# A hybrid SSD and attention block: z by seven block products, down's weight sums placed anew, other banks in the SSD stage

## The chip, the cores and the metric

One Trainium2 chip, one core of it. The time is that of the device for one execution of the whole kernel, in microseconds (us). Engines: PE (TensorE, matmuls; PEld is its weight load), DVE (VectorE), ACT (ScalarE), POOL (GpSimd), SP (SyncE, which here issues every DMA). The kernel before took 1809.08 us in the median of three runs (1808.15 to 1813.9).

## The reference

One layer of a decoder block on x of 1024 tokens by 1024 channels, in float32. Cut to what matters:

```python
h = rms_norm(x, pre_norm1_w) * (1 + sc1) + sh1
z, xbc, dt_raw, q, k, v, gates = split(h @ w_in)          # z: 1024 columns, dt_raw: 16
y_ssd = ssd_branch(z, xbc, dt_raw, ...)                   # Mamba-2, chunks of 128 tokens, 16 heads of 64
y_att = diff_attention_branch(q, k, v, ...)
merged = sigmoid(g_ssd) * (y_ssd @ w_ssd_o) + sigmoid(g_att) * (y_att @ w_attn_o)
x = x + g1 * rms_norm(merged @ w_out, post_norm1_w)
h2 = rms_norm(x, pre_norm2_w) * (1 + sc2) + sh2
u_gate, u_val = split(causal_dwconv(h2 @ w_up, ...))      # 2 x 2816 columns
x = x + g2 * rms_norm((gelu(u_gate) * u_val) @ w_down, post_norm2_w)

# in ssd_branch: y is the scan of xbc by dt, then
y = y * silu(z)
y = y * rsqrt(mean(y * y, over each of 2 groups of 512) + 1e-5) * norm_w
```

The block z with dt_raw, 1024 tokens by 1040 columns, inner length 1024, is what the first part of the change computes in another way.

## The kernel before, in words

**Arithmetic.** A large product is made in three matmuls: operands are split into a high and a low part (`split`, hi by ACT, lo by DVE's subtraction, L96), and hi·hi, hi·lo and lo·hi are summed in the same bank of PSUM.

**Order.** From the head to the end each of PE, DVE, ACT and SP runs its instructions in the order in which the program emits them (`manual_schedule`). An instruction that waits holds up everything behind it on its engine. On SP that holds for the issues of DMAs too: the issue of a load into a buffer that is still being stored waits for that store, and whatever stands behind it waits as well.

**Stages.** The head (norm of x, the first products) runs to about 92 us. Then come 15 **pairs**, m = 0 to 14, to 378.43 us. A pair makes two blocks of 128 columns of w_in times all tokens as 2x2 blocks in seven products p = 0 to 6 (Strassen, in Winograd's form). The right operands are fixed for all pairs: the four quarters of h and four sums of them (`b11`, `b21`, `t2`, `t1`, `t3`, `b22`, `t4`, in this order), kept split in `HX`. The left ones are weights and four sums of weights (`x_sum`, L406), split by `x_split` (L397 on ACT, L398 on DVE) three products ahead. A product is 12 matmuls of 128x512 (`x_mms`, L422 to L424). It goes to bank X, Z or Y; X is evicted by ACT copies and its sums with the others by DVE (L782, L791, L795). The last product, p = 6, writes into bank X, which L791 must have read. The kinds of the pairs set what else is done: gates (a tanh and a store), rope for q and k (pairs 1 and 3, posted one and two pairs later: swaps of rows by DMA, L468 and L469, and four DVE steps of 128x1024, L471 to L475), and in m = 10 to 14 the SSD input, whose causal convolution follows one pair later as DVE steps of up to 1.28 us (L499) and ACT steps (L496, L501).

**down's weight sums.** The feed-forward's last product uses seven block products too; the sums of its weights are made early, and go back to memory. `down_sums` (L533 to L543) makes four sums of 128x512 for each of 11 blocks of rows, two loads (L529) before and two stores after (L536, L543): 44 sums on DVE, 22 loads and 22 stores on SP. There are two sets of buffers (`wdr`). In the kernel before, 16 sums stand in pairs 10 to 14 (pair 10 after products 3 to 6, the others after 0, 3 and 6) and 28 in the z stage.

**z.** The 1040 columns are cut in thirds (346, 346, 348), and for each third eight tiles of 128 tokens are made by 24 matmuls (`mm3`, L117 to L119), 576 in all. The tokens are PE's stationary side, and the weights' columns move. A tile is evicted by ACT's tanh (L970) and a DVE step (L971) that gives twice silu(z), and is stored (L972); the factor goes into `nwr` and the norm. Beside that run the last pair's convolution, the end of ada (`ada_end`, `ada_turn`), down's sums, and the decays: `decays_a` (softplus of dt, L856 to L882), `decays_b` (cumulative sums by two matmuls, L886 to L893), `decays_c` (transposes of them and their store, L895 to L902).

**SSD.** Sixteen steps u (chunk c, group g). In a step: transposes of the inputs into a pair of banks (`ps_mm`, L1123 to L1134), the decay matrix M loaded (`load_decay`), made on ACT (L1147, L1149) and masked on DVE (L1154), the state's part `pq` (L1161), read by DVE (L1162), and the inner part `py` (L1165), read by DVE (L1167), then the state (`pst`, L1179). Steps later the normed y is turned by four transposes, `ytr` (L1220). Matmuls of v (L1051 to L1053) fill PE between them. Before, `pq` has bank wc, and `py` and `ytr` share bank wb. Attention, the dense part and the feed-forward follow; nothing changes in them but line numbers.

Of the kernel before, what the change touches and what calls it, by code (L numbers as in the profile page):

```python
# [17 lines left out]
P = 128  # L18
D = 1024
# [44 lines left out]
def kernel(ctx: ExitStack, tc: tile.TileContext, a: dict, out: bass.AP, dbg=None):  # L64
# [238 lines left out]
    zd = [dp.tile([P, D], F32, tag=f"zd{i}", name=f"zd{i}") for i in range(8)]  # L303
# [51 lines left out]
    thirds = ((0, 346), (346, 346), (692, 348))  # L355
    z_raw, wz = [], []

    def fetch_z(c0, wdt, kp):
        raw = zraw[:, :, :wdt] if kp == 3 else wp.tile([P, 2, wdt], F32, tag="wraw", name=f"wz{c0}_{kp}_raw", bufs=3)
        SP.dma_start(raw, a["w_zdt"][2 * kp * P : (2 * kp + 2) * P, c0 : c0 + wdt].rearrange("(k p) c -> p k c", p=P))  # L360
        return raw

    def split_z(c0, wdt, kp, raw, own=None):
        if own is not None:
            hi, lo = [t[:, :, :wdt] for t in own]
            split(hi, lo, raw)
            return hi, lo
        hi = wp.tile([P, 2, wdt], F32R, tag="whi", name=f"wz{c0}_{kp}_hi", bufs=4)
        lo = wp.tile([P, 2, wdt], F32R, tag="wlo", name=f"wz{c0}_{kp}_lo", bufs=4)
        split(hi, lo, raw)  # L370
        return hi, lo
# [58 lines left out]
    growt = const("growt", [2 * KD, P])  # L430
# [94 lines left out]

    def down_load(k, i):
        if k < KF:
            r0 = (k + KF * i) * P
            SP.dma_start(wdr[k % 2][i].rearrange("p h c -> p (h c)"), a["w_down"][r0 : r0 + P, :])  # L529

    def down_sums(k):
        (b11, b12), (b21, b22) = [(t[:, 0, :], t[:, 1, :]) for t in wdr[k % 2]]
        V.tensor_tensor(b11, b12, b11, op=ALU.subtract)  # L533
        yield
        V.tensor_tensor(b12, b22, b12, op=ALU.subtract)
        SP.dma_start(wtd[0][:, k, :, :], wdr[k % 2][0])  # L536
        if k > 0:
            down_load(k + 1, 1)
        yield
        V.tensor_tensor(b22, b22, b11, op=ALU.subtract)  # L540
        yield
        V.tensor_tensor(b21, b21, b22, op=ALU.subtract)
        SP.dma_start(wtd[1][:, k, :, :], wdr[k % 2][1])  # L543
        down_load(k + 2, 0)
        yield

    def all_sums():
        for k in range(KF):
            yield from down_sums(k)

    wdr = []
    sums_dn = all_sums()

    EN = mybir.EngineType
    with tc.manual_schedule(engines={EN.PE, EN.DVE, EN.Activation, EN.SP}):
# [199 lines left out]
        for m, (kind, *_) in enumerate(pairs):  # L755
# [6 lines left out]
            for p in range(7):  # L762
# [51 lines left out]
                if (m, p) in ((9, 4), (10, 3)):  # L814
                    wdr.append([SL.get(f"wdr{len(wdr)}{j}", F32, (P, 2, HALF)) for j in range(2)])
                if (m, p) in ((9, 4), (9, 5), (10, 3), (10, 4)):
                    down_load(*divmod(((9, 4), (9, 5), (10, 3), (10, 4)).index((m, p)), 2))
                if p in {10: (3, 4, 5, 6)}.get(m, (0, 3, 6) if m > 10 else ()):
                    next(sums_dn)
                if last:  # L820
                    SL.put(*HX[order[p][0]]) if order[p][0][0] == "t" else None
                    if p == 4:
                        for k in range(KH):
                            hT[k][1] = new_hl(f"b12_{k}")
                            SP.dma_start(hT[k][1].rearrange("p h t -> p (h t)").bitcast(F32), h12d[k])
                    if p == 3:
                        SL.put(*sab)
                    if p == 3:
                        zraw = SL.get("zraw", F32, (P, 2, HALF))
                    z_raw += [fetch_z(*thirds[0], kp) for kp in {1: (0,), 2: (1,), 3: (2, 3)}.get(p, ())]  # L830
                    for _ in range(max(0, p - 4)):
                        wz.append(split_z(*thirds[0], len(wz), z_raw.pop(0)))
# [109 lines left out]
    with tc.manual_schedule(engines={EN.PE, EN.DVE, EN.Activation, EN.SP}):  # L942
        for t_, (c0, wdt) in enumerate(thirds):
# [4 lines left out]
            for i in range(8):  # L948
# [24 lines left out]
                if t_ == 1 and i < 5:  # L973
                    dec = dec or decays_a()
                    for _ in range(6):
                        next(dec, None)
# [1660 lines left out]
```

## Time and profile before

| what | us |
|---|---|
| median of three runs (lowest, highest) | 1809.08 (1808.15, 1813.9) |
| the profiled execution | 1808.36 |
| its span | 1806.5 |
| pairs, with the 15 products of seven | about 92 to 378.43 |
| one pair | 19.05 to 19.10 |
| z | 378.43 to 471.28 |
| SSD | 471.28 to about 645 |

Rows of instructions give the start in us, the duration in us, the engine, the line, the operation, output and inputs, then the size (for PE first the stationary one); in brackets stands how long the engine was idle before it and what released it. PE's rows overlap: the next matmul starts before the modelled end of the last, so PE's pace is read from start to start. DVE's and ACT's rows overlap by a little too when they stand back to back (a sum of 0.69 adds 0.60). Windows give busy us and the instructions of each engine in a stretch.

### The profile page before, as it was taken

How to read it: one execution, taken by the hardware profiler on the slowest of the kernel's cores; microseconds unless marked ns; L12 is line 12 of the kernel's file. 1: busy time of each engine (PE TensorE's matmuls, PEld its weight loads, DVE VectorE, ACT ScalarE, POOL GpSimd, SP SyncE). 2: the span in 40 equal slices, each digit the busy share in tenths (PEclk: the TensorE clock that was granted, in tenths of full speed). 3: DMA queues.
4: the chain of work that ended last, by engine and by line, in shares of the span. 5: the costliest groups of instructions: out<-in, count | busy, mean ns of one | idle time of the engine just before them, and what ended most of it. 6: DMA issues, size and time to landing. Idle time of an engine off the chain costs nothing.

```text
span 1806.5 us, 24511 instructions
## 1 busy us (share of the span) xinstructions
PE 1780.1 (99%) x8749; PEld 1492.9 (83%) x8749; DVE 1362.5 (75%) x2245; ACT 919.8 (51%) x1794; POOL 111.2 (6%) x110
## 2 busy tenths in 40 slices
PE   8999999999999999999999999999999999999998
PEld 6788888899877788888888888888888888888887
DVE  7896888876488777666667877679898888876545
ACT  4454444442456656665555443665554554564532
POOL 0000000000155300000000000100000000000001
PEclk9999999999999999999999999999999999999999
DMA  9565787578877886679952576413232223378754
GB/s 373 174 222 165 254 276 254 181 241 285 263 247 234 251 251 171 183 198 279 262 153 99 178 247 256 157 55 117 96 127 104 100 99 111 122 239 301 238 158 165
DMA packets 165322, 356.18 MB, mean 197 GB/s; under 512 B 16064, under 2 KB 64976, under 8 KB 165200
## 3 DMA queue, kind: packets, MB, share of 16 engines
q1 hardware_dynamic: 165200, 354.62, 59.9%
q8 instruction: 69, 1.13, 0.3%
q14 instruction: 53, 0.43, 0.1%
HBM read 248.83 MB, written 103.62 MB: 195 GB/s over the span
## 4 chain that ended last, share of the span: by engine, by line
PE 54%; DVE 5%; DMA 3%; ACT 3%; issue 1%; SPq 0%; POOL 0%; DVEq 0%; POOLq 0%; ACTq 0%
PE upx L2025 4%; PE upx L2026 4%; PE upx L2024 4%; PE o L1531 2%; PE upy L2025 2%; PE upy L2024 2%; PE upy L2026 2%; PE dx L2416 2%; PE dx L2417 2%; PE dx L2415 2%; PE dy L2417 2%; PE dy L2415 2%; PE dy L2416 2%; PE mix L2087 1%; PE mix L2085 1%; PE mix L2086 1%
## 5 line engine op out<-in xcount | busy, mean ns | idle before, releaser
L2024 PE MATMUL upx<-t,wu_t 128*128 128x512 f32 x264 | 103.1, 391 | 0.5 <-DVE cv L2480 0.4
L2025 PE MATMUL upx<-t,wu_t 128*128 128x512 f32 x264 | 102.8, 390 | 0.2 <-DVE t L2142 0.2
L2026 PE MATMUL upx<-t,wu_t 128*128 128x512 f32 x264 | 102.7, 389 | 0.0
L1456 DVE CUSTOM_DVE_ANT_0 sc<-sc,mw 128x256 f32<-128x256 f32 (+7 forms) x128 | 96.2, 772 | 8.6 <-PE sc L1469 7.2
L1998 ACT ACTIVATE wu_t<-sab 128x512 fp32r<-128x512 f32 x57 | 34.1, 627 | 127.7 <-DVE sab L2015 127.7
L1519 ACT COPY aT<-at 128x512 f32<-128x512 f32 (+2 forms) x96 | 45.9, 478 | 95.8 <-PE at L1518 95.6
L96 DVE TENSOR_TENSOR g_lo<-gst,g_hi 128x1024 fp32r<-128x1024 f32 (+1 forms) x42 | 47.5, 1134 | 49.5 <-ACT g_hi L95 49.0
L1531 PEld LDWEIGHTS o<-vt,aT 128*128 128x128 f32 x576 | 76.0, 191 | 5.6 <-ACT aT L1519 0.2
L1531 PE MATMUL o<-vt,aT 128*128 128x128 f32 x576 | 79.9, 275 | 0.0
L95 ACT ACTIVATE g_hi<-gst 128x1024 fp32r<-128x1024 f32 (+1 forms) x42 | 41.5, 990 | 66.1 <-DMA gst<-gld_s 38.3
L397 ACT ACTIVATE xw_t<-xsab 128x512 fp32r<-128x512 f32 x45 | 27.3, 627 | 93.5 <-DVE xsab L406 93.5
L422 PE MATMUL xx<-xt,xw_t 128*128 128x512 f32 x180 | 70.1, 390 | 0.0
L424 PE MATMUL xx<-xt,xw_t 128*128 128x512 f32 x180 | 70.0, 389 | 0.0
L423 PE MATMUL xx<-xt,xw_t 128*128 128x512 f32 x180 | 70.0, 389 | 0.0
L1468 PE MATMUL sc<-kst,qst 128*128 128x512 f32 (+2 forms) x192 | 66.1, 352 | 0.0
L1506 DVE RECIPROCAL rsm<-ssum 128x2 f32<-128x2 f32 x64 | 10.6, 166 | 72.8 <-ACT p L1497 39.6
L1469 PE MATMUL sc<-klo,qst 128*128 128x512 f32 (+2 forms) x192 | 63.3, 346 | 0.4 <-DMA klo<-kld 0.4
L2042 DVE SCALAR_TENSOR_TENSOR ug<-cg,vec,ug 128x1023 f32<-128x1023 f32 (+1 forms) x44 | 56.3, 1280 | 6.1 <-ACT ug L2041 5.3
L2002 DVE TENSOR_TENSOR wu_t<-sab,wu_t 128x512 fp32r<-128x512 f32 x57 | 39.3, 690 | 26.5 <-ACT wu_t L1998 26.5
L2024 PEld LDWEIGHTS upx<-t,wu_t 128*128 128x128 f32 x264 | 49.6, 188 | 11.7 <-DVE cv L2480 1.4
L2025 PEld LDWEIGHTS upx<-t,wu_t 128*128 128x128 f32 x264 | 49.6, 188 | 10.7 <-DVE t L2142 0.5
L1510 DVE SCALAR_TENSOR_TENSOR p<-p,coef,p 128x512 f32<-128x512 f32 (+2 forms) x96 | 56.5, 617 | 2.3
(580 smaller groups left out, 5794.8 us busy)
## 6 DMA issues: line engine op xcount, KB each, us to landing
adas<-in_w_ada SPq DMA_DIRECT2D x32, 512.0 KB, 6.2
wdr<-in_w_down SPq DMA_DIRECT2D x22, 512.0 KB, 4.9
wtd<-wdr SPq DMA_DIRECT2D x22, 512.0 KB, 3.6
wuf<-in_w_up SPq DMA_DIRECT2D x22, 512.0 KB, 3.5
gld_s<-gsum SPq DMA_DIRECT2D x22, 512.0 KB, 2.7
gst<-gld_s SPq DMA_DIRECT2D x20, 512.0 KB, 4.6
wdt_raw<-wtd SPq DMA_DIRECT2D x20, 512.0 KB, 4.9
wuv<-in_w_up SPq DMA_DIRECT2D x19, 512.0 KB, 3.6
```

The lines of the kernel that those rows point to most:

```text
L422: T.matmul(o, wh, xh_, start=(k == 0 and first), stop=False, skip_group_check=not first)
L423: T.matmul(o, wh, xl_, start=False, stop=False, skip_group_check=not first)
L424: T.matmul(o, wl, xh_, start=False, stop=(k == KH - 1), skip_group_check=not first)
L1456: V.tensor_tensor_reduce(out=sc, in0=sc, in1=mw[:, S - L :], scale=1.0, scalar=3.0e38, op0=ALU.add, op1=ALU.min, accum_out=col)
L1468: T.matmul(sc[:, n0:n1], qs_[s][:, tsl], ks_[s][:, n0:n1], start=True, stop=False)
L1531: T.matmul(po_of[j, grp][:, qi, :], at[:, k, :], vt[j % 2][:, kt, :], start=(kt == 0), stop=(kt == i))
L2024: T.matmul(out_, wh, xh_, start=(k == 0 and first), stop=False, skip_group_check=not first)
L2025: T.matmul(out_, wh, xl_, start=False, stop=False, skip_group_check=not first)
L2026: T.matmul(out_, wl, xh_, start=False, stop=(k == end), skip_group_check=not first)
L2415: T.matmul(o, gh[:, kk, tsl], wh, start=(k == 0 and not more), stop=False, skip_group_check=more)
L2416: T.matmul(o, gh[:, kk, tsl], wl, start=False, stop=False, skip_group_check=more)
L2417: T.matmul(o, gl[:, kk, tsl], wh, start=False, stop=(k == KF - 1), skip_group_check=more)
```

## The change

Three things.

**z in seven products.** The 1040 columns are two halves h, and each half is two groups g of 260 columns. For each group the four blocks of weights (half of the inner length by half of the columns), `a11` to `a22`, are loaded (`z_load`), four sums made on DVE (`z_sum`, 128x1040 each), and seven operands split (`z_split`). The token side is the seven operands in `HX` that the pairs leave behind, so it needs no sums. A product is 4 tiles of 128 tokens by 12 matmuls, so 2 × 7 × 48 = 672 matmuls of 260 columns take the place of 576 of 346 or 348. Banks: X and Y of four each, exchanged between the groups; ACT copies what is to be added (`z_keep`), DVE adds it to the other bank (`z_out`), and ACT's own silu gives the result, straight from PSUM for the last. dt is taken from the first 16 columns. Product 3 of the second group is made in two parts, with product 4's first two tiles between them. Exact silu makes the factor in `nwr` and in the norm go. Silu and Exp are of different tables, so there are more table loads: 4 more of them stand in this stage.

**down's sums anew.** Twelve in pairs 3 to 5, eighteen in pairs 10 to 14 (pair 10 after products 2 to 5, 11 to 13 after 1 to 4, 14 after 1 and 2), fourteen in z. In pairs 3 to 5 one set of buffers does, and in pairs 10 to 14 too.

**SSD.** `ytr` has bank wc, which was `pq`'s, and `pq` has a bank of the pair `ps_mm`. M's first three loads, `xch`'s loads and v's first splits are made in the z stage; the first load of z stands a little later, and the quarter of h that `HX` doesn't hold (b12) is loaded again at the end of z.

The diff, cut to its core:

```diff
+    down_at = {(2, 4): "l", (2, 6): "l", (3, 2): "s", (3, 3): "s", (3, 4): "s", (3, 5): "l", (3, 6): "s", (4, 0): "l", (4, 1): "s", (4, 2): "s", (4, 3): "s"}
+    down_at |= {(4, 4): "ls", (4, 5): "l", (4, 6): "s", (5, 0): "s", (5, 2): "s", (5, 4): "s"}
...
+    for m in (11, 12, 13):
+        down_at |= {(m, 1): "s", (m, 2): "s", (m, 3): "s", (m, 4): "ls", (m, 5): "l"}
...
-                if p in {10: (3, 4, 5, 6)}.get(m, (0, 3, 6) if m > 10 else ()):
-                    next(sums_dn)
+                down(down_at.get((m, p), ""))
...
+    def z_mms(g, p, qs=range(4)):
+        n, bk = order[p]
...
+        wh, wl = zop[7 * g + p]
+        for q in qs:
+            o = zbank[g, bk, q]
+            tsl = slice(q * P, (q + 1) * P)
+            for k in range(KH):
+                xh_, xl_ = HX[n][k][:, 0, tsl], HX[n][k][:, 1, tsl]
+                T.matmul(o, xh_, wh[:, k, :], start=(k == 0 and first), stop=False, skip_group_check=not first)
+                T.matmul(o, xh_, wl[:, k, :], start=False, stop=False, skip_group_check=not first)
+                T.matmul(o, xl_, wh[:, k, :], start=False, stop=(k == KH - 1), skip_group_check=not first)
...
+    def z_out(g, h, half, bk, e, o):
+        t = zout[o]
...
+            if e is None:
+                A.activation(t[:, q, :], zbank[g, bk, q], AF.Silu)
+            else:
+                V.tensor_tensor(t[:, q, :], zbank[g, bk, q], zev[e][:, q, :], op=ALU.add)
...
+        z_mms(1, 2)
+        z_keep(1, "X", 1)
+        assert next(dec, None) is None
+        decays_b()
+        z_split(12)
...
+        down("sss")
+        v_raw.append(fetch_v(0, 2))
+        z_mms(1, 3, (0, 1))
+        decays_c()
+        z_mms(1, 4, (0, 1))
+        z_keep(1, "Y", 0, (0, 1))
+        z_mms(1, 3, (2, 3))
...
-            pq = ps_wc(f"pq{c}_{g}")
+            pq = ps_mm(f"pq{c}_{g}")[:, 0, :]
...
-                turn_y(*divmod(u - 3, 2))
+                turn_y(*divmod(u - 3, 2), ps_wc)
```

Two places of DVE's order show what the list `down_at` and the new z stage do. The first is the second half of pair 13, from the sum of weights in product 1 to the eviction of bank X before product 6; `wdr` are down's sums, `xw_t` and `xw_b` the splits of weights, `xbcT` the convolution's steps, `xsab` the sums of weights, `xcg` and `xcv` the evictions. Before:

```order
L406 TENSOR_TENSOR xsab_797<-xwf_2533,xwv_2640 128x512
L398 TENSOR_TENSOR xw_t_2779<-xsab_797,xw_t_2779 128x512
L499 SCALAR_TENSOR_TENSOR xbcT_2761<-xcg_889,vec,xbcT_2761 128x1022
L782 TENSOR_TENSOR xcg_697<-xz_2743,xevs_888 128x512
L398 TENSOR_TENSOR xw_b_2798<-xsab_797,xw_b_2798 128x512
L499 SCALAR_TENSOR_TENSOR xbcT_2761<-xcg_889,vec,xbcT_2761 128x1021
L398 TENSOR_TENSOR xw_t_2816<-xwv_2640,xw_t_2816 128x512
L499 SCALAR_TENSOR_TENSOR xbcT_2819<-xcv_890,vec,xbcT_2819 128x1023
L542 TENSOR_TENSOR wdr_2275<-wdr_2275 128x512
L398 TENSOR_TENSOR xw_b_2838<-xwf_2677,xw_b_2838 128x512
L499 SCALAR_TENSOR_TENSOR xbcT_2819<-xcv_890,vec,xbcT_2819 128x1022
L791 TENSOR_TENSOR xcv_698<-xx_2742,xevs_888 128x512
```

And now, from the sum of product 1 (L540's first row here) on:

```order
L540 TENSOR_TENSOR wdr_2293<-wdr_2293 128x512
L792 TENSOR_TENSOR xcg_690<-xz_2763,xevs_881 128x512
L403 TENSOR_TENSOR xw_b_2818<-xsab_790,xw_b_2818 128x512
L503 SCALAR_TENSOR_TENSOR xbcT_2781<-xcg_882,vec,xbcT_2781 128x1021
L540 TENSOR_TENSOR wdr_2293<-wdr_2294,wdr_2293 128x512
L403 TENSOR_TENSOR xw_t_2838<-xwv_2656,xw_t_2838 128x512
L503 SCALAR_TENSOR_TENSOR xbcT_2841<-xcv_883,vec,xbcT_2841 128x1023
L540 TENSOR_TENSOR wdr_2294<-wdr_2294,wdr_2293 128x512
L403 TENSOR_TENSOR xw_b_2858<-xwf_2696,xw_b_2858 128x512
L503 SCALAR_TENSOR_TENSOR xbcT_2841<-xcv_883,vec,xbcT_2841 128x1022
L540 TENSOR_TENSOR wdr_2294<-wdr_2294 128x512
L801 TENSOR_TENSOR xcv_691<-xx_2762,xevs_881 128x512
```

Between the convolution's step of 1022 and the eviction there was one sum; now there are four, one after each of products 1 to 4.

The second place is DVE around the decays' end in z: `acum_ps` is the bank of the cumulative sums, `acs` the copies of their transposes, `wz` splits of z's weights. Before:

```order
L889 COPY sm_3039<-acum_ps 128x128
L892 TENSOR_TENSOR sm_3039<-acum_ps,sm_3039 128x128
L535 TENSOR_TENSOR wdr_2274<-wdr_2275,wdr_2274 128x512
L540 TENSOR_TENSOR wdr_2275<-wdr_2275,wdr_2274 128x512
L96 TENSOR_TENSOR wz_1_lo<-wz_1_raw,wz_1_hi 128x696
L96 TENSOR_TENSOR wz_2_lo<-wz_2_raw,wz_2_hi 128x696
L96 TENSOR_TENSOR wz_3_lo<-zraw,wz_3_hi 128x696
L971 SCALAR_TENSOR_TENSOR ev_3041<-ev_3041,z_7_3601 128x346
L542 TENSOR_TENSOR wdr_2275<-wdr_2275 128x512
L971 SCALAR_TENSOR_TENSOR ev_3042<-ev_3042,z_0_3644 128x348
```

And now:

```order
L889 SCALAR_TENSOR_TENSOR sm_3051<-sm_3051,aexp 128x128
L368 TENSOR_TENSOR wza_3261<-zxr,wza_3259 128x1040
L96 TENSOR_TENSOR wz1t_lo<-wza_3261,wz1t_hi 128x1040
L896 COPY sm_3051<-acum_ps 128x128
L899 TENSOR_TENSOR sm_3051<-acum_ps,sm_3051 128x128
L96 TENSOR_TENSOR wz1b_lo<-wza_3323,wz1b_hi 128x1040
L540 TENSOR_TENSOR wdr_2293<-wdr_2294,wdr_2293 128x512
L540 TENSOR_TENSOR wdr_2294<-wdr_2294,wdr_2293 128x512
L540 TENSOR_TENSOR wdr_2294<-wdr_2294 128x512
L908 COPY acs<-acT_ps_3763 16x512
```

The copy of `acum_ps` stands behind a sum and a split of 1040 columns, and the copies of the transposes behind a split and three sums of down; before, they stood several tiles of z apart. (The last row is the first of the two copies.)

More of the change, by code (lines that the diff above doesn't have):

```diff
@@ L547, in all_sums, with down_sum @@
[L547 to L552, printed above, removed]
+        r0 = (k + KF * i) * P
+        SP.dma_start(wset(k)[i].rearrange("p h c -> p (h c)"), a["w_down"][r0 : r0 + P, :])
+    def down_sum(k, i):
+        (b11, b12), (b21, b22) = [(t[:, 0, :], t[:, 1, :]) for t in wset(k)]
+        o, x_, y_ = ((b11, b12, b11), (b12, b22, b12), (b22, b22, b11), (b21, b21, b22))[i]
+        V.tensor_tensor(o, x_, y_, op=ALU.subtract)
+        if i % 2 == 1:
+            SP.dma_start(wtd[i // 2][:, k, :, :], wset(k)[i // 2])
@@ L1006 @@
+    assert n_ada == 32 and n_dn == 4 * KF
+    SL.put(*HX["t4"], *zev, *zout, zxr, *wdr[0], *wdr[1])
     singles.close()
@@ L1012 @@
     GW = HALF
-    RH = NH // 2
-    M = [SL.get(f"M{n}", F32, (P, RH, P)) for n in range(3)]
     yt = [SL.get(f"yt{i}") for i in range(3)]
```

311 lines of the change are left out of this document (181 added, 130 removed).

## The prediction

> **What bounds the kernel now.** I read the page's busy shares first, then the groups of waits on PE by stretch, then windows for the stretches that the change touches, then single rows.
>
> ```profile
> span 1806.5 us, 24511 instructions
> PE 1780.1 (99%) x8749; PEld 1492.9 (83%) x8749; DVE 1362.5 (75%) x2245; ACT 919.8 (51%) x1794; POOL 111.2 (6%) x110
> ```
>
> PE is busy 99% of the span, so time falls only where PE gets less work or loses one of its few waits. The waits of PE from the z stage into attention, as PE's line, what it waited for, total us, times, longest:
>
> ```profile
> PE ytr L1220 <- DVE yt L1167: 4.1, 3, 2.1
> PE py L1165 <- DVE M L1154: 0.6, 1, 0.6
> PE v L1052 <- DVE wv_lo L920: 0.4, 1, 0.4
> ```
>
> That is 5.1 us in the SSD stage. The pairs and z have none. Three windows follow: z, a late pair (m=13) and an early one (m=4). The columns are the stretch, its length, then busy us and instructions of PE, PEld, DVE, ACT, POOL, the granted clock, the DMA share and GB/s:
>
> ```profile
> 378.43:471.28 92.85, 92.85 (x591) 92.46 (x590) 56.36 (x108) 25.89 (x46) 0.00 (x0) 1.00 0.84 281
> 340.33:359.38 19.05, 19.05 (x85) 15.70 (x84) 17.07 (x24) 10.17 (x15) 0.00 (x0) 1.00 0.59 185
> 168.60:187.70 19.10, 19.10 (x86) 15.83 (x85) 13.10 (x18) 6.36 (x11) 0.00 (x0) 1.00 0.44 133
> ```
>
> In z, DVE works 56 of 93 us; in a late pair it works 17.1 of 19.05. So z has room on DVE and the late pairs have next to none, and the change takes sums out of z and puts two of them into pairs. That the clock is 1.00 everywhere leaves it out of what follows. The profiled execution took 1808.36 us, 1.9 outside its span; it lies 0.7 below the median of the runs shown (1809.08) and 0.2 above the lowest. I count from 1808.36. About 0.3%, 5.4 us, is what a measurement of this kernel can tell from no change: below 1802.9 is faster, above 1813.8 slower.
>
> **A. PE's work in z.** 576 matmuls of 346 or 348 columns go, 672 of 260 come.
>
> ```profile
> 378.43 0.32 PE L117 MATMUL z<-wz_hi,hT 128*128 128x346 f32 x1
> 471.12 0.32 PE L119 MATMUL z<-wz_hi,hT 128*128 128x348 f32 x1
> 749.26 0.28 PE L1468 MATMUL sc<-kst,qst 128*128 128x256 f32 x1
> 749.38 0.28 PE L1469 MATMUL sc<-klo,qst 128*128 128x256 f32 x1
> 749.50 0.40 PE L1468 MATMUL sc<-kst,qst 128*128 128x512 f32 x1
> ```
>
> Durations overlap, so what counts is the step from start to start. In z it is (92.85 − 1.5)/576 = 0.1586 us, with about 1.5 us for the 15 other PE instructions (591 − 576: transposes and sums of ada and the decays, at some 0.1 us each). No row shows 260 columns; 256 columns step 0.12 (749.26, 749.38, 749.50), 346 columns 0.1586. By the slope between these, 0.0004 a column, 260 would be 0.1217; by the 256-wide rows in proportion 0.1219; read to their two digits, 0.118 to 0.123. I take 0.120, since rounding hides a few ns: 672 × 0.120 = 80.6 us (79.3 to 82.7). With the same 1.5 that is 82.1, or −10.7 before any wait.
>
> The product (14,6), of twelve 512-wide matmuls, goes from 375.71 to 378.43 (the rows below), 0.2267 each. The Trainium skill, TensorE: Matmul & The Clock Gate, section "Wait — 56ns, not 53.3ns?", gives N ÷ 2.4 GHz and about 2.5 ns from start to start, which is 0.216 for 512 columns, 0.147 for 346 and 0.111 for 260; the sum by it would have 74.5 us instead of 80.6. The rows here are 5 and 8% above it, so the measurement decides.
>
> **B. New waits in z.** Before, z needs from DVE only weight splits and evictions with whole tiles to spare. After, PE's 12-matmul groups stand in one order with transposes of the decays, whose inputs stand on DVE behind splits, and with banks that DVE must empty. Prices of what stands in the queues, on DVE and ACT:
>
> ```profile
> 461.64 1.22 DVE L920 TENSOR_TENSOR zown<-wv_raw,zown 128x1024 fp32r<-128x1024 f32 x1
> 495.38 0.42 DVE L1086 TENSOR_TENSOR was<-was 128x256 f32<-128x256 f32 x1
> 448.85 1.27 DVE L901 COPY acs<-acT_ps 16x512 f32<-16x512 f32 x2
> 413.01 0.46 ACT L970 ACTIVATE ev<-z 128x346 f32<-128x346 f32 x1 [0.71 <-PE z L119]
> 413.49 1.28 ACT L858 ACT_TABLE_LOAD   x1
> 414.78 0.31 ACT L858 ACTIVATE sm<-sm 128x128 f32<-128x128 f32 x1
> ```
>
> DVE's sum there is no bound: 22 splits and sums of 1040 columns at 1.22, 24 adds of 260 at 0.42 and 14 down sums at 0.69 make 47 us; with the last conv steps and the decays some 70 of 86. The waits are of order. Product 3 of the second group is cut in two, and its tiles 2 and 3 take the banks of the two transposes. Their copies (1.27 together) stand behind a weight split (1.22) and three down sums (3 × 0.60 in a row): 4.3 us on DVE from the moment the subtraction before them is done. PE has tiles 0 and 1 of product 4 to do meanwhile, 24 × 0.12 = 2.9. That leaves 1.4, with hand-over 1.6. The transposes before them wait for the copy of acum, which stands behind a 1040-wide sum and split: 1.0; the second half of the decays' chain runs over ACT, where table loads of 1.28 now stand: 1.0. The cumulative sums wait 0.4 for la, the ada transposes 0.3 for gcol. Sum 4.3. Lower bound 1, if DVE runs ahead by one split (1.2) at each of them; upper bound 7, if it is a split late at each of two. A + B: −6.4, from −11 to −2.
>
> The trace shows the load at 413.49 start 0.02 after the ACTIVATE before it ended and last 1.28, and the next operation follows at 414.78: 1.3 us a switch. The Trainium skill, ScalarE: Activation LUTs, section "What ACT_TABLE_LOAD costs", gives about 1283 ns and about 1380 ns of drain for each switch; the load agrees, and no row here shows a drain.
>
> **C. Down's sums in pairs 11 to 14.** There were three in a pair (products 0, 3, 6); now four (products 1 to 4), and two in pair 14.
>
> ```profile
> 339.12 0.69 DVE L795 TENSOR_TENSOR xcg<-xy,xevs 128x512 f32<-128x512 f32 x1
> 341.71 0.69 DVE L535 TENSOR_TENSOR wdr<-wdr,wdr 128x512 f32<-128x512 f32 x1
> 344.18 1.28 DVE L499 SCALAR_TENSOR_TENSOR xbcT<-xcg,vec,xbcT 128x1023 f32<-128x1023 f32 x1 [0.58 <-ACT xbcT L496]
> 355.76 0.68 DVE L791 TENSOR_TENSOR xcv<-xx,xevs 128x512 f32<-128x512 f32 x1
> 358.76 0.69 DVE L795 TENSOR_TENSOR xcg<-xy,xevs 128x512 f32<-128x512 f32 x1
> 374.80 0.69 DVE L791 TENSOR_TENSOR xcv<-xx,xevs 128x512 f32<-128x512 f32 x1
> 375.71 0.39 PE L422 MATMUL xx<-xt,xw_t 128*128 128x512 f32 x1
> ```
>
> PE's last product of a pair reuses the bank that L791 (L801 after) empties. In pair 13 the eviction ends at 356.44, and PE starts that product at 359.38 − 2.72 = 356.66: 0.22 to spare. In pair 14 it ends at 375.49 against 375.71: 0.22 again. DVE's own period is 358.76 − 339.12 = 19.64 against PE's 19.05, so in pair 12 there was 0.8 to spare and in pair 11 1.4: DVE falls behind by 0.6 a pair already, and nobody notices until it has used its lead. After, the sum at 341.71, which lay in front of a wait for ACT of 0.58 anyway, is gone, and two sums stand where DVE never waits: 2 × 0.60 = 1.2 more a pair, a period of 20.85. Pair 11 uses up its lead of 1.4. By pair 12 DVE is 2 × 1.2 = 2.4 later, less some 0.5 that it still idled for ACT in pair 11, against 0.8: PE waits 1.1. From then on the bound is DVE's period: 20.85 − 19.05 = 1.8 in pair 13. Pair 14 has two sums and no longer the third, but one split of z's weights (1.15) stands before the eviction: 1.15. Sum +4.1; less if ACT's lag eats the sums (3), 5 if every sum counts. The cover that is gone is DVE's lead; once PE is stalled, what is late next is z's second product, whose split stands behind the same row; PE has 5.8 us of product 0 before that.
>
> **D. Sums in pairs 3 to 5.** Twelve sums, six loads and six stores are put among the swaps, stores and weight loads of the rope pair on SP. The first three rows are of DVE, the next two are groups of DMAs with count, KB each and us from issue to landing; then the spread of the loads and of everything on that tile:
>
> ```profile
> 168.42 0.69 DVE L398 TENSOR_TENSOR xw_t<-xsab,xw_t 128x512 fp32r<-128x512 f32 x1 [0.70 <-ACT xw_t L397]
> 178.46 0.69 DVE L398 TENSOR_TENSOR xw_t<-xwv,xw_t 128x512 fp32r<-128x512 f32 x1 [2.58 <-ACT xw_t L397]
> 183.08 0.68 DVE L791 TENSOR_TENSOR xcv<-xx,xevs 128x512 f32<-128x512 f32 x1
> wdr<-in_w_down SPq DMA_DIRECT2D x22, 512.0 KB, 4.9
> wtd<-wdr SPq DMA_DIRECT2D x22, 512.0 KB, 3.6
> DMA to landing us min/median/max: 4.1/4.9/7.3
> DMA to landing us min/median/max: 2.8/4.5/8.2
> ```
>
> There is only one set of buffers here, so a block's second load follows its predecessor's store. The last sum of block 0 ends at 169.7 (behind the row at 168.42), its store lands 3.6 later, 173.4, SP issues the load behind it at 173.9, it lands at 178.8. DVE comes to sum (4,2) at about 175.9, in the 2.58 that it idled before 178.46, so it stands there 2.9, and rope's three steps of 1.22 and the eviction of 183.08 are behind it. That eviction ended at 183.76, and PE's product 6 starts at 187.70 − 2.72 = 184.98, so 1.2 of the 2.9 is covered; some of the rest the later idle time takes. PE waits 0.4 to 1.2 there, and 0 to 2.5 in pair 5, where an eviction on ACT stands behind rope's copy and that behind DVE. Swap DMAs issue up to 3 us later, behind the down load that waits; rope's steps follow them. I take +1.5, from 0 (the loads land at 4.1 and the idle time holds all) to 4. Pairs 10 and z's own loads have two products' time, 5.4 us, or more after the store.
>
> **E. SSD's banks.** The rows are of PE, DVE and ACT:
>
> ```profile
> 517.39 0.66 PE L1220 MATMUL ytr<-ident,yt 128*128 128x128 f32 x4 [2.06 <-DVE yt L1167]
> 558.51 0.66 PE L1220 MATMUL ytr<-ident,yt 128*128 128x128 f32 x4 [1.42 <-DVE yt L1167]
> 589.38 0.66 PE L1220 MATMUL ytr<-ident,yt 128*128 128x128 f32 x4 [0.67 <-DVE yt L1167]
> 515.45 0.68 DVE L1162 TENSOR_TENSOR tt<-pq,sm 128x512 f32<-128x512 f32 x1
> 516.65 0.68 DVE L1167 TENSOR_TENSOR yt<-py,yt 128x512 f32<-128x512 f32 x1
> 478.81 1.28 ACT L1147 ACTIVATE M<-M,sm 128x128 f32<-128x128 f32 x4 [3.40 <-DMA M<-acd]
> ```
>
> ytr waits for L1167 because it takes py's bank; the data that it turns are two steps older. With the wc bank it needs none of this. pq now stands in the mm pair, which L1162 frees 1.2 us ahead of L1167, so the next user of the pair can wait for that where ytr waited: 2.06 − 1.2 = 0.9 in the worst of the three, 1.42 − 1.2 = 0.2 in the next, nothing in the last; but v's matmuls stand between in some steps, so 0.4. M's loads are issued in z, so ACT's 3.40 and PE's 0.6 behind it go, and the 0.4 of v too. −4.1 + 0.4 − 0.6 − 0.4 = −4.7, from −5.1 to −2.5 (M stays, and a half of ytr's wait moves to the pair).
>
> **Sum.** −6.4 + 4.1 + 1.5 − 4.7 = −5.5: 1808.4 − 5.5 = 1802.9, written 1803.0.
>
> **The rivals.** *PE alone bounds.* If sums and new waits find idle time after all (C at 0, D at 0, B at 1), −9.7 − 4.7 gives 1794; with one of the three still there 1796 to 1799. For it: DVE's busy share is 75%. Against it: 0.22 us of slack in two late pairs. Chance 0.22.
>
> *Shorter steps at 260 columns.* By the figure of the page on TensorE above, 6.1 less than my sum: 1797; the 512- and 346-wide rows speak against it: 0.04.
>
> *DVE takes PE's place.* C 5, D 4, B 6: −4.7 + 5 + 4 − 4.7 = −0.4, 1808. For it: the period of 19.64 in the late pairs. Against: that 75%. 0.17.
>
> *A drain at each table switch.* Two of the new loads stand on the way of the decays; if ACT paused after each as long again as its load, 1.3, the transposes would be 2.6 later: 1805.5. The page on ScalarE above names such a drain; the row at 414.78 speaks against it: 0.03.
>
> *Down's loads come late (slower).* Each block's second load waits for a store to land. At the longest landings, 8.2 and 7.3, a block has 15.5 us between sum and sum, where pairs 4 and 5 leave 6 and pairs 11 to 13 about 13. Then DVE stands 9 us at each of two blocks, 18, of which idle time and lead take some 6, so D is 12 instead of 1.5; and 2.5 at each of three blocks of the late pairs, where no lead is left, 7.5. Together 18 over the forecast: 1821. It turns slower than before at 11 us over the forecast, 2.2 us for each of the five. For it: nothing but those maxima; the medians, 4.9 and 3.6, leave only D's 2.9. 0.08.
>
> That the change doesn't do what it says I leave out: the program has the 672 matmuls.
>
> **How the numbers follow.** Forecast 0.46, half of it on either side of 1802.9 (own range 1799 to 1807). So faster 0.23 + 0.22 + 0.04 = 0.49; same 0.23 + 0.17 + 0.03 = 0.43; slower 0.08. The range, 1795 to 1811, leaves out the late loads and a third of the case of PE alone.
>
> **What would show it.** Right: 260-wide steps of 0.12, z at 84 to 88 us, PE waits at product 6 of pairs 12 to 14 of 1 to 2 us each for L801, one at pair 4 or 5, ytr's wait gone. Wrong: no wait in the late pairs (C falls), a z of 82 (B falls) or over 90, waits on wdr's loads of over 3 us in pairs 10 to 13, or new waits on the mm pair of over 2 us.

## The result and the profile after

The changed kernel takes 1831.58 us in the median of five runs (1830.73 to 1835.97), the kernel before 1809.24 (1808.15 to 1813.9): a ratio of 1.0124, interval 1.011 to 1.0139. The forecast was 1803. The profiled execution took 1830.73, its span:

```profile
span 1828.9 us, 24673 instructions
PE 1798.2 (98%) x8845; PEld 1485.6 (81%) x8845; DVE 1377.8 (75%) x2248; ACT 935.9 (51%) x1814; POOL 111.7 (6%) x110
```

PE is busy 18 us more than before, though the z stage was to take 10 us of work from it. So the first question is not which wait came, but where PE's work got longer. I set the starts of the same matmuls in the two traces side by side and took the growth of each stretch, in us:

| stretch | before | change |
|---|---|---|
| up to the first pair | 92.55 | +0.46 |
| pairs 0 to 3 | 76.40 | +1.16 |
| pairs 4 to 6 | 57.12 | +5.41 |
| pairs 7 to 11 | 95.20 | +1.77 |
| pairs 12 and 13 | 38.12 | +2.87 |
| pair 14 and z | 111.89 | −5.51 |
| SSD, to the last ytr | 173.08 | +1.37 |
| attention | 354.43 | −1.41 |
| dense part to the feed-forward | 167.53 | +3.11 |
| feed-forward, to the last matmul | 633.66 | +13.30 |

The feed-forward, in which no instruction changed, is 13.3 us longer, and the pairs 7 to 9, unchanged too, are about 0.4 longer each. Here are 100 us of the feed-forward, as in the windows of the prediction. Before:

```profile
1310.00:1410.00 100.00, 100.00 (x443) 82.80 (x442) 86.62 (x114) 52.23 (x77) 0.00 (x0) 1.00 0.31 109
```

And after:

```profile
1310.00:1410.00 100.00, 100.00 (x433) 80.99 (x433) 86.59 (x114) 49.04 (x73) 0.00 (x0) 1.00 0.32 113
```

Both rows say 100 us busy and a clock of 1.00, and no wait. Only the count differs: 443 matmuls before, 433 after. From start to start the 512-wide ones take 0.2267 us before and 0.2318 after on average, 2.2% more. It is so from the first pair (0.231) to the end, with one exception: in attention the 512-wide matmuls of the dense products that fill PE take 0.2303 before already (0.2319 after), and attention isn't longer. It is not in any list of waits, since a matmul that takes longer counts as busy. The waits that the trace does list for PE, from the groups of the whole span:

```profile
...
PE v L1157 <- ACT zout L988: 2.9, 1, 2.9
PE xx L427 <- DVE xcv L801: 2.4, 3, 1.0
PE xx L427 <- ACT xevs L795: 2.4, 1, 2.4
PE pq L1262 <- DVE prev L1282: 1.4, 1, 1.4
...
PE acT_ps L907 <- DVE sm L899: 1.1, 1, 1.1
...
PE acT_ps L907 <- DVE sm L896: 0.9, 1, 0.9
...
PE z L975 <- DVE acs L908: 0.2, 1, 0.2
```

ytr's wait for L1167 is gone, and so is the one for M, as forecast; the pairs and z have the waits that terms B to D spoke of; and the SSD stage has two new ones, 2.9 us for ACT's last silu of z and 1.4 for DVE's sum of the state.

### The profile page after: what moved, and what is told of

It reads as the page before. It is cut to its first block, busy times and chain, and to the rows that moved or that the text cites. A ratio compares the mean times of both kernels' runs of the same rounds, so it can differ in the third digit from the quotient of the medians.

```text
span 1828.9 us, 24673 instructions
## 1 busy us (share of the span) xinstructions
PE 1798.2 (98%) x8845; PEld 1485.6 (81%) x8845; DVE 1377.8 (75%) x2248; ACT 935.9 (51%) x1814; POOL 111.7 (6%) x110
## 3 DMA queue, kind: packets, MB, share of 16 engines
q8 instruction: 70, 1.15, 0.3%
## 4 chain that ended last, share of the span: by engine, by line
PE 65%; DVE 3%; ACT 2%; DMA 1%; issue 1%; POOL 0%; DVEq 0%; SPq 0%; POOLq 0%; ACTq 0%
PE upx L2124 4%; PE upx L2123 4%; PE upx L2122 4%; PE o L1629 3%; PE dx L2515 2%; PE dx L2514 2%; PE dx L2513 2%; PE upy L2124 2%; PE upy L2123 2%; PE upy L2122 2%; PE dy L2515 2%; PE dy L2513 2%; PE dy L2514 2%; PE at L1616 2%; PE mix L2185 1%; PE mix L2184 1%
## 5 line engine op out<-in xcount | busy, mean ns | idle before, releaser
L2122 PEld LDWEIGHTS upx<-t,wu_t 128*128 128x128 f32 x264 | 49.6, 188 | 12.2 <-DVE cv L2578 0.6
L2123 PEld LDWEIGHTS upx<-t,wu_t 128*128 128x128 f32 x264 | 49.6, 188 | 12.0 <-DVE t L2240 0.5
L2124 PEld LDWEIGHTS upx<-t,wu_t 128*128 128x128 f32 x264 | 49.6, 188 | 11.6
```

The lines of the kernel that those rows point to most:

```text
L2122: T.matmul(out_, wh, xh_, start=(k == 0 and first), stop=False, skip_group_check=not first)
L2123: T.matmul(out_, wh, xl_, start=False, stop=False, skip_group_check=not first)
L2124: T.matmul(out_, wl, xh_, start=False, stop=(k == end), skip_group_check=not first)
```

## The experiments

**What slows PE.** Two theories. The first: where the operands lie. A weight tile of z is 4 × 260 × 4 = 4160 bytes a partition, and the pools give each buffer of a tag the size of its largest tile. So the 11 weight buffers, and five of the 43 slots behind them, grow by 64 bytes, and everything behind each moves. In the program as built, all that PE reads for a 512-wide matmul (all but 4 of some 6,400) began, before, at one residue of its address modulo 512, and now at many residues, 64 bytes or a multiple of it apart. The rival: the new instructions themselves, or the load that they put on the chip. One kernel takes the bytes away from the changed kernel (z256), two give them to the kernel before (pad_all, pad_raw).

z256:

```diff
-    ZW = (D + NH) // 4
+    ZW = 256
...
+        if (g, h) == (1, 1):
+            SP.dma_start(zdh[half][:, :, D - NH :], t[:, :, ZW - NH :])
```

> The changed kernel with groups of 256 columns instead of 260; it leaves out the last 16 columns of z and stores a copy of other columns there. Every operand tile is 4096 bytes a partition again, so all tiles begin at one residue of the address modulo 1024, as before the change; everything else stays. Theory 1 (the 64 bytes by which the 4160-byte tiles push their neighbours cost PE a slower step, 0.2317 us instead of 0.2267 a 512-wide matmul, everywhere): about 1800 to 1806 us, with the step back at 0.2267 in the pairs and in the feed-forward. Rival (the slower step comes with the new instructions, their number or the load they put on the chip): 1829 us, the step stays at 0.232, since only 672 x 4 columns, about 1 us, are left out.

Measured: 1812.23 us (8 runs, 1810.2 to 1815.37) beside 1808.3 for the kernel before on this chip, a ratio of 1.0022 (1.001 to 1.0034). The same 100 us:

```profile
1310.00:1410.00 100.00, 100.00 (x443) 82.85 (x442) 87.26 (x117) 51.18 (x75) 0.00 (x0) 1.00 0.32 113
```

The step is back, with 672 new matmuls still there. The time is some 6 us over what I expected of it, which the waits below account for.

pad_all, the opposite (the same for the tags of the high and low parts):

```diff
-        t = xw[n, m] = wp.tile([P, 2, KH, P], F32, tag="wraw", name=f"xw{n}{m}", bufs=3)
+        t = xw[n, m] = wp.tile([P, 1040], F32, tag="wraw", name=f"xw{n}{m}", bufs=3)[:, :D].rearrange("p (n k c) -> p n k c", n=2, c=P)
```

> The kernel before with the tiles of the three weight tags (raw, high, low) made 4160 bytes instead of 4096, which nothing reads, and two small constants placed in a tile that exists; no instruction changes. Theory 1 (addresses): step 0.230 to 0.232 us, 1825 to 1838 us. Rival (new instructions): 1808 to 1810 us, step 0.2267.

Measured: 1828.06 us (two runs), ratio 1.011 (1.0081 to 1.014), no instruction added:

```profile
1310.00:1410.00 100.00, 100.00 (x436) 81.65 (x435) 86.56 (x114) 48.12 (x72) 0.00 (x0) 1.00 0.32 111
```

So the bytes alone do it, and the rival falls.

pad_raw makes only the three raw buffers larger:

> The kernel before with only the three raw weight tiles made 4160 bytes: nearly all that PE reads moves by 192 bytes together and keeps one residue modulo 1024 (896 instead of 704). If theory 1 holds because the operands no longer share a residue: no change, 1808 to 1810 us, step 0.2267. If it is the residue itself that counts: about 1830 us. Rival (new instructions): 1808 to 1810 us.

Measured: 1808.23 us, step 0.2267. Everything was moved by 192 bytes, but together. It isn't the residue that counts, but that it is shared.

**How much must be shared.** Two kernels that compute all of z, and differ only in the size of the 260-column tiles. Room came from constants that were put into tiles that exist (the masks, the rows for lambda, four small ones).

```diff
-        hi = wp.tile([P, KH, ZW], F32R, tag="whi", name=f"wz{g}{n}_hi", bufs=4)
+        hi = wp.tile([P, 1088], F32R, tag="whi", name=f"wz{g}{n}_hi", bufs=4)[:, : KH * ZW].rearrange("p (k c) -> p k c", c=ZW)
```

The low parts and the five slots are made so too; in aligned128 1056 stands for 1088.

> The changed kernel whole, all 1040 columns, with its 260-column tiles given 4352 bytes (17 x 256) instead of 4160, so that every operand of PE begins at one residue modulo 256 again; room for it comes from constants placed in tiles that exist. Theory 1 (a tile's address relative to the others sets PE's step, and a residue shared modulo 256 is enough): step 0.2265 to 0.228 us, 1810 to 1815 us. If only a residue shared modulo 1024 helps: step 0.231, about 1830 us. Rival (the 260-column matmuls themselves slow everything): about 1830 us.

> The kernel with aligned tiles, at 4224 bytes (33 x 128) instead of 4352, so that operands share a residue modulo 128 but not modulo 256; no instruction changes. If the residue modulo 256 is what PE's step hangs on: step 0.229 to 0.232 us, 1822 to 1832 us. If modulo 128 is enough: 0.2267, 1811 to 1815 us.

Measured: aligned 1813.09 us (10 runs), ratio 1.0025 (1.0015 to 1.0036); aligned128 1830.67 in one run. Their windows, first aligned:

```profile
1310.00:1410.00 100.00, 100.00 (x443) 82.88 (x442) 87.27 (x116) 49.95 (x74) 0.00 (x0) 1.00 0.31 108
```

And aligned128:

```profile
1310.00:1410.00 100.00, 100.00 (x434) 81.25 (x433) 86.99 (x114) 50.58 (x75) 0.00 (x0) 1.00 0.31 111
```

With tiles of 4352 bytes, 17 × 256, the step is whole; with 33 × 128 it is lost. The change was 22.3 us slower than before, aligned is 4.5, each against the kernel before on its own chip: 17.8 us are this. What all five kernels of this kind move is tiles, which PE reads and the other engines and the DMAs read and write. That PE's own reads are what counts is the likeliest reading, not shown by itself; the last section has what speaks for it.

**The rest: what is left of the change at the old pace.** aligned is still those 4.5 us slower than before, where the forecast had −5.4. The 256-column kernel shows the waits at the old pace. Its groups of waits for PE, from 100 to 500 us:

```profile
PE xx L427 <- DVE xcv L801: 4.1, 3, 1.8
PE xx L427 <- ACT xevs L795: 2.9, 1, 2.9
PE z L975 <- DVE acs L908: 1.7, 1, 1.7
PE acT_ps L907 <- DVE sm L899: 1.1, 1, 1.1
PE acT_ps L907 <- DVE sm L896: 0.5, 1, 0.5
...
```

Three kernels undo one place each. z256_early (the twelve sums of pairs 3 to 5 left out):

```diff
-    down_at = {(2, 4): "l", (2, 6): "l", (3, 2): "s", (3, 3): "s", (3, 4): "s", (3, 5): "l", (3, 6): "s", (4, 0): "l", (4, 1): "s", (4, 2): "s", (4, 3): "s"}
-    down_at |= {(4, 4): "ls", (4, 5): "l", (4, 6): "s", (5, 0): "s", (5, 2): "s", (5, 4): "s"}
...
+        for k in range(6):
+            SP.dma_start(wtd[k % 2][:, k // 2, :, :], wdr[1][k % 2])
```

> The 256-column kernel (it leaves out 16 columns of z) without the twelve sums of down in pairs 3 to 5, their loads and stores; it leaves those sums out and stores other rows in their place at the end of z. Theory (term D is 3 us or more, since loads and a slot wait for stores to land): PE's waits of 2.9 us in pair 5 and 1.8 in pair 6 go, start of z 4 to 5.5 us earlier than in the 256-column kernel, 1805 to 1808 us in all. Rival (PE's time there is lost to the rope steps anyway): start of z at most 1 us earlier.

z256_late (it loads the next block's rows one sum too early, so some of down's sums are of other rows; the work is the same):

```diff
-    for m in (11, 12, 13):
-        down_at |= {(m, 1): "s", (m, 2): "s", (m, 3): "s", (m, 4): "ls", (m, 5): "l"}
-    down_at |= {(14, 1): "s", (14, 2): "s"}
+    down_at |= {(m, p): "s" for m in (11, 12, 13, 14) for p in (0, 3, 6)}
+    down_at |= {(11, 5): "l", (12, 1): "l", (13, 0): "sl", (13, 4): "l", (14, 2): "l"}
...
+        down("l")
...
+        down("ss")
```

> The 256-column kernel with down's sums in pairs 11 to 14 at products 0, 3 and 6, as before the change, and the two sums that are then over put into z. Theory (term C: two sums more a pair on DVE's path, 4.1 us): the three waits on the last product of pairs 12 to 14, 4.1 us, shrink to under 0.5, z starts 3.5 to 4.5 us earlier. Rival (DVE is late because of pairs 3 to 10 or of z's own splits): at least 2 us of the waits stay.

z256_order:

```diff
         decays_b()
-        z_split(12)
...
-        down("sss")
...
         decays_c()
+        z_split(12)
+        down("sss")
         z_mms(1, 4, (0, 1))
```

> The 256-column kernel with one weight split and three of down's sums put behind the copies of the decays' transposes instead of ahead of them. Theory (term B: the copies queue behind them): the wait of 1.7 us of z's matmuls for the copies goes, z 1.5 to 2 us shorter. Rival (the wait then moves to the split, or the transposes' own waits for acum of 1.1 and 0.5 grow): z shorter by less than 0.5.

Measured: 1813.12, 1810.97 and 1811.3 us, one run each. The first is above the 1805 to 1808 expected of it, for a reason that comes with the SSD stage; the totals say little, the growth over before by stretch does:

| stretch | z256 | early | late | order |
|---|---|---|---|---|
| up to the first pair | +2.46 | +0.23 | +0.06 | +2.47 |
| pairs 4 to 6 | +5.38 | 0.00 | +6.96 | +6.80 |
| pairs 12 and 13 | +2.98 | +3.00 | −0.02 | +2.96 |
| pair 14 and z | −6.21 | −6.22 | −5.63 | −8.17 |
| SSD | −1.77 | +7.65 | −1.44 | −1.11 |

The first two edits take their own places to nothing, the third takes 2.0 off z: the early sums cost 5.4 to 7.0, the late ones 3.0 in two pairs, the copies' queue 2.0. Where the early sums cost more than 5.4, the clock differs too: where pairs 4 to 6 lost 6.8 or 7.0 us (order 6.8, late 7.0, and 6.8 in aligned), the granted clock was 0.50 for 3.4 or 6.8 us in and behind the wait in pair 5; where they lost 5.4 (z256 and the changed kernel), it stayed at 1.00. In z256_late:

```profile
201.90:208.70 6.80, 5.54 (x13) 4.38 (x14) 4.26 (x7) 3.27 (x7) 0.00 (x0) 0.50 0.91 336
```

The expectation for the late pairs had one of the three waits for xcv in the wrong place: the longest, 1.8, stands in pair 6 and went with the early sums. (The first row differs by up to 2.4 between executions of the same instructions, so totals of single runs are read with care.) What made the early sums so dear shows in DVE's waits in the 256-column kernel, from 150 to 240 us, and in SP's:

```profile
...
DVE xql L492 <- DMA wtd<-wdr: 5.9, 1, 5.9
DVE wdr L540 <- DMA wdr<-in_w_down: 4.1, 2, 2.1
...
```

```profile
SPq L535 <- DMA wtd<-wdr: 12.3, 3, 5.0
...
```

The loads do wait behind stores, as term D had it (4.1 us on DVE). But the longest, 5.9, is another: the buffers of down's sums go back to the slots in pair 5, pair 6 gets one of them for its split of q, and DVE's first write there waits for the last store. PE's two waits match these: 2.9 us stand in pair 5, behind the loads and the rope steps that follow them, and 1.8 in pair 6, behind the slot. No edit is aimed at one of the two alone.

And z256_early's SSD stage, 7.65 us longer with six extra stores at the end of z, pointed to the third loss.

**The SSD stage.** The banks alone, in the kernel before:

```diff
-            pq = ps_wc(f"pq{c}_{g}")
+            pq = ps_mm(f"pq{c}_{g}")[:, 0, :]
...
-                turn_y(*divmod(u - 3, 2))
+                turn_y(*divmod(u - 3, 2), ps_wc)
```

> The kernel before with the SSD stage's banks alone changed (the turned y in wc, pq in the mm pair); M is still loaded late. My term E by itself: the three waits of 4.1 us for the inner part's reading go and about 0.4 comes back, so 1804 to 1806 us. Rival (the wait moves to the mm pair or to the state's reading): 1807 to 1809 us with a new wait of 1 to 4 us on pq or px.

> The kernel before with the SSD banks alone, timed against it: 1805 to 1807 us, faster than before by 0.1 to 0.2%; the SSD stage 5 us shorter, about 2 us of it given back in attention. Rival (the first look was chance): 1808 to 1810 us.

Measured: 1806.22 in one run beside 1808.3; then 1805.61 (10 runs), ratio 0.9978 (0.9969 to 0.9987). The stage is 5.26 and 5.14 us shorter, and of its waits this is left, from 470 us on:

```profile
...
PE v L1052 <- DVE wv_lo L920: 0.4, 1, 0.4
PE px L1123 <- DVE tt L1162: 0.3, 1, 0.3
```

So the banks do what term E said, in full. In aligned the same banks gain nothing (+1.13), nor in the changed kernel (+1.37). There PE's waits in the stage are the 2.9 and 1.4 us listed above (4.6 with a small one), and behind the first the clock is halved for 3.4 us, which at half pace is an estimated 1.7 lost:

```profile
482.20:485.60 3.40, 3.40 (x10) 2.63 (x9) 2.55 (x2) 3.38 (x8) 1.61 (x1) 0.51 1.03 399
```

ACT's last silu, for which PE waits 2.9 us, stood behind two splits of v and then for z's own store of the tile that it writes, from 470 to 485 us:

```profile
ACT zout L988 <- DMA zd<-zout: 1.6, 1, 1.6
```

That wait was not tried by itself; in aligned it is 0.4, and the loss is elsewhere. There DVE stands for this, from 478 to 525 us:

```profile
DVE was L1192 <- DMA was<-in_w_attn_o: 5.4, 1, 5.4
...
```

and, right behind, two windows of the stage:

```profile
510.00:520.00 10.00, 7.00 (x30) 4.53 (x29) 9.86 (x16) 6.09 (x17) 5.67 (x5) 1.00 0.72 216
520.00:529.00 9.00, 9.00 (x36) 7.00 (x35) 7.52 (x12) 0.17 (x2) 3.23 (x3) 0.62 0.93 337
```

In the first PE is idle for 3 us of 10; in the second it is busy throughout, but the granted clock is 0.62, and 36 instructions pass where aligned_light, below, has 49. The idle time is paid twice. These loads of attention's weights stand on SP behind the last stores of down, whose sums the change put at z's end. aligned_light leaves the last two blocks of down out there:

```diff
-        down_load(9, 0)
...
-        down_load(9, 1)
-        down("ll")
...
-        down("ss")
...
-        down("ss")
...
-        down("ssss")
         new_b12((2, 3))
```

> The kernel with aligned tiles, without the last two blocks of down in z: eight sums, four loads and four stores are left out (other rows are stored much later in their place). Theory (SSD's gain is lost because stores and loads at the end of z hold up SP's queue, so that the loads for attention's weight sums land late and DVE stands): the wait of 5.4 us of DVE for those loads goes, PE's waits of 1.3 and 1.5 us for DVE go, the granted clock stays at 1.00 through the SSD stage, which is 5 to 6 us shorter: about 1806 to 1808 us. Rival (the new banks only move the waits): the SSD stage is at most 1 us shorter.

Measured: 1807.15, and the SSD stage 6.49 us shorter than before. Its windows, the same stretches:

```profile
510.00:520.00 10.00, 10.00 (x57) 8.02 (x56) 9.83 (x17) 4.96 (x14) 4.50 (x5) 1.00 0.97 338
520.00:529.00 9.00, 9.00 (x49) 7.13 (x48) 7.08 (x12) 6.64 (x18) 6.99 (x6) 1.00 0.63 171
```

DVE's wait for these loads is gone, and the clock holds. The run takes eight sums from DVE as well as the transfers; z256_early, which has six stores more at this place and not one sum more, shows that the transfers are enough: there DVE stands 14.5 us for the same loads, and the clock is at 0.50 for 10.2 us. SP issued the first of the loads at 488.95, 12.1 us into the stage; in aligned at 497.15, 18.9 into it:

```profile
488.95 2.60 SPq L1179 DMA_DIRECT2D was<-in_w_attn_o  x4
```

```profile
497.15 3.46 SPq L1186 DMA_DIRECT2D was<-in_w_attn_o  x4
```

**All together.** The experiments point to a version with shared residues and down's sums at places that wait for nothing. Only a sketch of the diff, which moves lists:

```diff
+    down_at = {(2, 4): "l", (2, 6): "l", (3, 2): "s", (3, 3): "s", (3, 4): "s", (3, 6): "s"}
...
+    down_at |= {(11, 1): "s", (11, 3): "s", (11, 6): "s", (12, 0): "ls", (12, 1): "l", (12, 3): "s", (12, 6): "s"}
...
-        down("ssss")
         new_b12((2, 3))
...
+        wdr[:] = [[SL.get(f"wdr{i}{j}_", F32, (P, 2, HALF)) for j in range(2)] for i in range(2)]
+        down("llll")
```

> The kernel with aligned tiles (4352 bytes) and down's 44 sums placed a third way: four in pair 3, sixteen in pairs 10 to 14 at products 0, 3 and 6 (or beside them), twelve in z and none at its end, twelve in the dense stage after attention; in z the split and the three sums stand behind the copies of the transposes. Theory: terms A, B and E come out once C and D are gone and no late store stands on SP before the SSD stage: 1813 less 5 to 6.8 (D), 4 (C), 2 (order) and 3 to 5 (SSD): 1796 to 1802 us, faster than the kernel before by 0.4 to 0.7%. Rival (the sums cost DVE and SP as much wherever they stand): 1808 to 1814 us, with new waits in the dense stage.

Measured: 1800.47 us (5 runs, 1799.13 to 1803.51) beside 1810.1 on its chip, ratio 0.9952 (0.9938 to 0.9966): faster than both kernels. By stretch: up to the first pair, which differs between executions, +2.2, pairs 0.0, pair 14 and z −6.01, SSD −1.08, attention and all behind −0.6. Its waits for PE, from 100 to 480 us:

```profile
PE v L1153 <- ACT zout L984: 2.0, 1, 2.0
PE acT_ps L903 <- DVE sm L895: 1.1, 1, 1.1
PE acT_ps L903 <- DVE sm L892: 1.1, 1, 1.1
...
```

None is left in the pairs. The SSD stage still lost 4 of its 5 us. PE's waits in it, then SP's from 466 to 502 us:

```profile
PE v L1153 <- ACT zout L984: 2.0, 1, 2.0
PE pq L1258 <- DVE prev L1278: 1.5, 1, 1.5
PE px L1225 <- DVE tt L1259: 0.7, 2, 0.4
```

```profile
SPq L1216 <- DMA zd<-zout: 5.2, 1, 5.2
...
SPq L1311 <- DMA wtd<-wdr: 3.1, 1, 3.1
...
```

Half of it is the last silu again. The other half comes behind a wait of 4.6 us of DVE for the same loads of attention's weights, which SP issued 19.5 us into the stage: ahead of them it waited 3.1 us for a store of down and 5.2 for a store of z. What would give these 4 us too wasn't tried.

## Why the prediction was wrong

**The sum itself.** It added five terms to 1808.4, and so took for granted that every matmul that the change leaves alone keeps its step of 0.2267. That failed, and by itself makes about 18 of the 28.6 us between 1803.0 and 1831.6. The prediction read the 0.2267 off the rows as a property of 512 columns; the runs show that, outside attention, it is one of 512 columns in a program whose operands share a residue modulo 256 (0.231 to 0.232 otherwise). Nothing in the profile of before could show that, as it has next to no operand elsewhere; but the size of the new tiles, 4160 bytes in pools of 4096, was in the diff, and it was not costed at all. The Trainium skill, SBUF — State Buffer, section "Operand start alignment", asks of an operand only that it starts at a multiple of its element size, and says that this "is about legality, not speed"; all the kernels here obey that, and those with mixed starts are 1.1 to 1.2% slower. Most signs that the prediction named for being right did come (260-wide steps of 0.12, z of 85.9 us, a wait in pair 5, ytr's wait gone; of the waits in the late pairs one reached 1 us), and none of them looks at a matmul that the change leaves alone.

**A** was right: 672 matmuls at 0.120 were forecast, and the steps of the 260-column matmuls average 0.120 in the changed kernel, where the clock is full and PE doesn't wait. The step of 0.111, which the Trainium skill, TensorE: Matmul & The Clock Gate, section "Wait — 56ns, not 53.3ns?", would give, did not come.

**B** was right in its places and nearly in size: 1.0 and 1.0 were forecast for the two transposes, 1.1 and 0.9 came; 1.6 for the copies, 1.7 came in the 256-column kernel, and moving what stands ahead of the copies gave 2.0 back. In the changed kernel the copies' wait is 0.2, for a reason that the step did not count. Behind the waits of 0.9 and 1.1 the granted clock falls, in windows of the changed kernel:

```profile
453.00:456.00 3.00, 1.84 (x11) 1.37 (x12) 0.29 (x1) 2.63 (x6) 0.00 (x0) 0.82 0.99 252
456.00:458.30 2.30, 2.30 (x13) 2.30 (x13) 2.22 (x3) 0.55 (x3) 0.00 (x0) 0.50 0.85 310
```

In the second, matmuls of 260 columns step 0.217 instead of 0.120. That is about 1.3 us more, and it takes the place of the copies' wait: PE comes to them later. The Trainium skill, TensorE: Matmul & The Clock Gate, section "What's actually happening", has the clock set by recent activity of PE, over windows of about 3.4 us; the 0.50 agrees with its lower state, and here it fell behind 2.0 us of idle time within 2.6 (452.2 to 454.8). It did not fall behind 1.6 us in two waits in the 256-column kernel, nor behind 2.2 at the same place in aligned_light, so that the idle time alone doesn't tell.

**C** was right in mechanism and size where it was measured: 1.1 and 1.8 us in pairs 12 and 13 were forecast, the pairs are 1.24 and 1.74 us longer in the 256-column kernel (waits of 0.9 and 1.5 and what follows them), and both went with the old places. In pair 14, forecast 1.15, the program as built puts seven matmuls of z ahead of the last product, so PE fills most of that wait; the front part's sentence that every engine runs in the order of the program text is too strong there.

**D** was mis-sized: 1.5 (0 to 4) was forecast, 5.4 to 7.0 came. The wait on the late loads was as described; two things were missing. The wait that follows in pair 5 was put at 0 to 2.5 and is 2.9, with a slower clock behind it in some executions; and the slot, with 1.8 in pair 6, was not seen: the step looked for who reads down's buffers, and not for who gets them next.

**E** was right by itself (−4.7 forecast, −5.2 with the banks alone) and failed in the whole: in aligned it is +1.1. The step said that M's loads are issued in z and left it there. It did not count what else the change issues on SP at the same place, four stores and four loads of down, behind which attention's loads stand, and not that the first matmuls of v would wait for ACT's last silu.

Of the rivals, "down's loads come late" comes nearest in kind, since D and the loss in SSD are both stores that hold up what stands behind them on SP; but it named other pairs, and its price was not what made the kernel slower. No rival had PE's step in it.

## What to carry to other kernels

When a change alters the size of a buffer, compare the addresses of everything behind it, not only the instructions; a tile padded to a multiple of 256 bytes cost nothing here, and 64 bytes too many cost 1%. When work that the change doesn't touch gets longer, count matmuls in equal windows: a slower step shows as busy time and in no list of waits. And a store that is moved to a place with room on its engine is costed by who gets its buffer and by what stands behind it on the queue.

## What the runs showed of the hardware

- PE's step for 512 columns, outside attention: 0.2267 us when all operands start at one residue modulo 256, 0.231 to 0.232 when they are multiples of 64 or 128 bytes apart; moving all of them by 192 bytes together changes nothing. In pad_all, where the moving operands of the feed-forward's first product all keep one residue, matmuls whose stationary operand has it too modulo 256 step 0.2274 and 0.2285, the others 0.230 to 0.233. In aligned128, where both vary, matmuls whose two operands share it step 0.230 on average and the others 0.232, and none is back at 0.2267 as a group; in the changed kernel the two groups differ by less than 0.001. So it isn't a matter of one matmul's two operands alone. Why that is stays open; nothing here shows what in PE or in the memory is shared. In attention the dense products' steps are 0.2303 with a shared residue too, and that is open as well.
- In 90 us of the feed-forward (1310 to 1400) every step of the kernel before is 226 or 227 ns, an even pace; with mixed starts, in the changed kernel, nearly all lie spread between 224 and 241 ns.
- The granted clock, where it falls within a kernel, is 0.50 for 3.4, 6.8 or 10.2 us at a time (in the changed kernel twice 3.4, at 454.9 and 482.2; in aligned 6.8 at 521.2; in z256_early 10.2 at 505.0), in or behind waits of PE of 1.5 us or more in one piece or two. The wait alone doesn't decide it: ytr's wait of 2.06 us at 517 left the clock at 1.00 in the kernel before, and in pad_raw it fell to 0.50 behind the same wait of 2.05.
- Gains in front of attention are partly lost in it: the banks alone save 5.2 us by the end of the SSD stage, and attention is 2.0 and 1.65 longer. This was seen in two executions, and its cause wasn't tried.
